# Mixer of a two-layer diffusion backbone: two attention heads side by side on halves of the array, projections ranked ahead, no modulation dots in the mixer

## The chip, the cores and the metric

The kernel runs on one core of one Trainium2 chip. The metric is device time in microseconds of that core for one launch; lower is better. The core's engines are TensorE (PE in the profile, with PEld for its weight loads), VectorE (DVE), ScalarE (ACT), GpSimd (POOL) and SyncE (SP, which issues the DMAs). They run beside each other, each through its own queue in order, and are tied together by semaphores.

## The reference, cut to what matters

There are 256 latent tokens and 256 context tokens, 1024 features and two layers. Layer 0 is a half-step SwiGLU, then a mixer of windowed attention and a gated linear attention (GLA), then another half-step SwiGLU. Layer 1 is a SwiGLU, a pooling mixer, a SwiGLU. Each norm is modulated by columns that come from a conditioning vector: nine vectors of 1024 a layer, each a matrix-vector product. The change lies in the mixer of layer 0 and in the place of some of those products.

```python
def adaln(cond, w, b):                       # 9 modulation vectors of 1024 for a layer
    mm = jax.nn.silu(cond) @ w + b
...
def window_attention(q, k, v, kc, vc, sink): # 8 query heads of 64, 2 key/value heads of 64
    s_band = jnp.einsum('bnigrd,bnjgd->bgrnij', qb, kb).astype(jnp.float32) * scale
    s_ctx = jnp.einsum('bnigrd,blgd->bgrnil', qb, kc).astype(jnp.float32) * scale
    s_band = jnp.where(valid, s_band, -jnp.inf)
    p = jax.nn.softmax(jnp.concatenate([s_band, s_ctx, sink_l], axis=-1), axis=-1)
    o = (jnp.einsum('bgrnij,bnjgd->bnigrd', p[..., :nk], vb)
         + jnp.einsum('bgrnil,blgd->bnigrd', p[..., nk:nk + L], vc))
...
def gla_chunked(q, k, v, log_a, s0):         # 4 heads of 64 x 128, chunks of 64, both directions
    g = jnp.cumsum(chunks(log_a), axis=2)
    q_t = qc_ * jnp.exp(g)
    k_t = kc_ * jnp.exp(-g)
    att = jnp.where(lower, jnp.einsum('bnihd,bnjhd->bnhij', q_t, k_t), 0.0)
    o = jnp.einsum('bnhij,bnjhv->bnihv', att, vc_)
    ...
    o = o + jnp.einsum('bnihd,bnhdv->bnihv', q_t, s_prev)
```

## The kernel before, in words

Activations lie feature by token: 128 features on the partitions, 256 tokens along the free axis. Weights come from HBM in blocks of 128 x 1024 (512 KB). `weight` (L139 to L146) loads such a block into one of four `raw` buffers, ScalarE casts it to `hi` (L144), and VectorE subtracts to get `lo` (L145); each product is then three matmuls (`product`, L327 to L329, on 258 columns; `wide`, L342 to L344; `merged`, L336 and L337). The matmuls inside the mixer that concern this change are plain fp32 matmuls; the trace shows two records for each of them.

The stages follow one another: the two-stream SwiGLU of layer 0 (`ffn_two`), the mixer (`mixer`), the second SwiGLU of layer 0 and the first of layer 1 (`ffn_one`: 22 blocks p of two weights, then eight output blocks), the pooling mixer, the last SwiGLU. In `ffn_one` the blocks p below 9 use `product` and the later ones `wide`.

A modulation column is made by a *dot*: VectorE multiplies a 128 x 1024 weight tile by the conditioning row and sums it (L174). `queue_mod` lists the dots in order; `step_mod(rate)` does so many of them per step of a stage and keeps two loads ahead. In the SwiGLUs the weight tiles go into two buffers of their own (`rawm`); in the mixer they use the four `raw` buffers. The rates of the second SwiGLU of layer 0 and the first of layer 1 are the first two pairs of `RATES` (dots for each block p from 5 on, and for each output block). In the mixer one dot follows each projection named in `DOTS`: ten in all.

The mixer's order of work is written by a small planner, `Flow`. Each piece of work is a generator; `step(pe, post, needs, sets)` tells the planner what it costs on PE, which VectorE ("D") and ScalarE ("A") work follows, and which events it needs and sets. The planner always continues the ready task with the lowest rank (`RANK`), and a task whose `post` work is not done is not ready. The order that comes out is then laid on the engines by the recording layer, which moves some instructions of its own. The tasks are:

- `project`: 19 blocks of the input projection (`ORDER`), each one or two times 24 matmul records of `product`, then L374 on VectorE and L766 on ScalarE;
- `gate`: decays, and from them `k_t`, `q_t` (GLA keys and queries); `q_t` has one slot a head, its other 64 rows zero;
- `scores(d, tb)`: GLA scores, four 128 x 128 matmuls a call over all 128 rows (L971);
- `states`: GLA states (L951), two heads on the two halves of the array's columns, alternating;
- `gla_head`: a head's output, per half of the tokens one L984, four L989 (64 columns each, all 128 rows), one L991; then its norm, which goes through a matmul of ones (L999);
- `attend(j, g, qb, u)`: one head and one query block: scores (L904, 128 x 512, `k_g` zero in the other head's 64 rows), VectorE (L907 to L909), ScalarE (L910, L911), VectorE (L912 to L914), four transposes (L921), a ScalarE copy (L922), and after the second query block four value matmuls (L931) into the half of a bank that belongs to the head's group g. There are 16 of them, and three P buffers (`PBUF`) let three be under way;
- `output`: eight output blocks with `merged`.

Of the kernel before, what the change touches and what calls it, by code (L numbers as in the profile page):

```python
# [13 lines left out]
ALU = mybir.AluOpType  # L14
# [44 lines left out]
RANK = dict(gate=0, small=1, scores=3, states=3, gla=2, attend=2, output=5, project=10)  # L59
# [47 lines left out]
class Body:  # L107
# [597 lines left out]
    def mixer(self, cur, nxt):  # L705
# [12 lines left out]
        k_g = t(lp, [128, 2, 512])  # L718
        k_t = t(lp, [128, 2, 2, T])
        q_t = t(lp, [128, 2, 4, T])  # L720
# [4 lines left out]
        for z in (k_g, q_t, KT):  # L725
            nc.gpsimd.memset(z, 0.0)
# [67 lines left out]
        def rope(blk):  # L794
# [7 lines left out]
            if blk == "ka":  # L802
                for g in (0, 1):
                    r = slice(g * 64, g * 64 + 64)
                    nc.vector.tensor_tensor(k_g[r, g, :T], t1[r], t2[r], op=ALU.add)
                    nc.scalar.copy(k_g[r, g, T:], z[r, T:])
            else:
                nc.vector.tensor_tensor(q_r[:, int(blk[2]), :], t1, t2, op=ALU.add)
# [13 lines left out]
        def gate(d, b):  # L822
# [32 lines left out]
            for hh in (0, 1):  # L855
                r = slice(hh * 64, hh * 64 + 64)
                nc.vector.scalar_tensor_tensor(out=q_t[r, d, 2 * b + hh, :], in0=Z[f"qb{b}"][r], scalar=0.125,
                                               in1=ep[r], op0=ALU.mult, op1=ALU.mult)
# [37 lines left out]
        pv_bank, pv_last, PT = {}, {}, {}  # L896

        def attend(j, g, qb, u):


            h = g * 4 + j
            sk = self.cols[:, C_SK + h:C_SK + h + 1]
            ps = self.bank()
            nc.tensor.matmul(ps, q_r[:, j, qb * 128:(qb + 1) * 128], k_g[:, g, :], start=True, stop=True)  # L904
            p = t(sp, [128, 512], F32, "P", PBUF)
            st = t(sp, [128, 4], F32, "st", 4)
            nc.vector.tensor_tensor_reduce(out=p, in0=ps, in1=band[:, qb, :], scale=0.125, scalar=sk,  # L907
                                           op0=ALU.add, op1=ALU.max, accum_out=st[:, 0:1])
            nc.vector.tensor_scalar_mul(st[:, 1:2], st[:, 0:1], -1.0)  # L909
            nc.scalar.activation(st[:, 3:4], sk, AF.Exp, bias=st[:, 1:2])  # L910
            nc.scalar.activation(p, p, AF.Exp, bias=st[:, 1:2], accum_out=st[:, 2:3])  # L911
            nc.vector.tensor_tensor(st[:, 2:3], st[:, 2:3], st[:, 3:4], op=ALU.add)  # L912
            nc.vector.reciprocal(st[:, 2:3], st[:, 2:3])
            nc.vector.tensor_scalar_mul(p, p, st[:, 2:3])  # L914
            yield step(0.86, [("D", ATT[0]), ("A", ATT[1]), ("D", ATT[2])])
            if qb == 0:
                PT[h] = t(sp, [128, 4, T], F32, "PT", 2)
            pt = PT[h]
            pk = self.bank()
            for kb in range(4):  # L920
                nc.tensor.transpose(pk[:, kb * 128:(kb + 1) * 128], p[:, kb * 128:(kb + 1) * 128], self.ident)  # L921
            nc.scalar.copy(pt[:, :, qb * 128:(qb + 1) * 128], pk.rearrange("p (k q) -> p k q", q=128))  # L922
            yield step(0.44, [("A", 0.48)], sets=[f"T{u}"])
            if qb == 0:
                return
            if j not in pv_bank:
                pv_bank[j] = self.bank()
            po = pv_bank[j]
            with self.after(pv_last.get(j)):
# [112 lines left out]
        for d in (0, 1):  # L1042
            for tb in (0, 1):
                flow.add(RANK["scores"], scores(d, tb), [f"qk{d}0", f"qk{d}1"])
# [243 lines left out]
```

## Time and profile before

| what | us |
|---|---|
| median of 3 runs (1159.35 to 1163.1) | 1162.02 |
| the profiled execution: its own time | 1161.4 |
| the profiled execution: span of its instructions | 1159.2 |
| PE busy | 1137.5 |
| DVE busy | 938.5 |
| ACT busy | 587.4 |
| mixer, from the first projection on PE to the start of the next SwiGLU's blocks | 391.87 to 564.11 |
| second SwiGLU of layer 0, `product` blocks, then `wide` blocks | 564.11 to 618.48, to 693.35 |
| first SwiGLU of layer 1, `product` blocks, then `wide` blocks | 755.54 to 807.78, to 882.65 |

The span runs from the first to the last instruction; 2.2 us of the execution lie outside of it. The granted TensorE clock is full (0.997 in the mean). In a row of the timeline the first number is the start, the second the length up to the modelled end of the last instruction, and "xN" counts records; since matmuls are pipelined, the cost of a block is the distance from its start to the start of what follows. Rows of groups give the busy sum, the mean of one instruction in ns, and the idle time before them with what ended it. A row of the windows gives the stretch, its length, and for PE, PEld, DVE, ACT and POOL the busy time in it with the count of instructions; then the clock, the DMA engines' share and GB/s.

### The profile page before, as it was taken

The page shows a single profiled execution, that of the slowest core. Times are in us where ns is not written, and L with a number is a line of the kernel's source. Part 1 is how long each engine was busy: PE and PEld are TensorE (multiplying, and loading weights), DVE is VectorE, ACT ScalarE, POOL GpSimd, SP SyncE. Part 2 cuts the span into 40 slices and gives each one's busy share as a digit, 9 for nine tenths or more (in the row PEclk, how much of TensorE's full clock was granted, in tenths as well). Part 3 has the DMA queues.
Part 4 walks back from the last instruction along what each step waited for, and adds up shares of the span by engine and source line. Part 5 has one row for each costly group of instructions (what it writes and reads, how often), then busy time and mean ns, then how long its engine had stood idle before and what let it go on. Part 6 is the DMA issues. An engine that isn't in the chain of part 4 may idle for free.

```text
span 1159.2 us, 19546 instructions
## 1 busy us (share of the span) xinstructions
PE 1137.5 (98%) x7450; PEld 1027.0 (89%) x7450; DVE 938.5 (81%) x1662; ACT 587.4 (51%) x999; POOL 9.9 (1%) x32
## 2 busy tenths in 40 slices
PE   7999999999999999999999999999999999999997
PEld 5899988888888899787999998899999889988886
DVE  6899899787758889776999877989886889967664
ACT  4547645323234474565574444565544556556543
POOL 0000000000000200000000000000000000000000
PEclk9999999999999999999999999999999999999998
DMA  9867557667866535321759977868996864756562
GB/s 332 289 243 240 164 179 233 198 217 243 249 191 191 171 108 177 115 69 54 234 187 324 326 236 246 283 208 284 340 312 203 261 226 147 252 185 192 153 185 88
DMA packets 74544, 247.42 MB, mean 213 GB/s; under 512 B 8273, under 2 KB 8913, under 8 KB 74194
## 3 DMA queue, kind: packets, MB, share of 16 engines
q1 hardware_dynamic: 74450, 246.17, 64.4%
q8 instruction: 58, 0.95, 0.3%
q14 instruction: 36, 0.29, 0.1%
HBM read 245.09 MB, written 1.05 MB: 212 GB/s over the span
## 4 chain that ended last, share of the span: by engine, by line
PE 86%; DVE 7%; DMA 3%; ACT 2%; issue 2%; SPq 0%; DVEq 0%; ACTq 0%
PE t_mm L336 15%; PE t_mm L342 11%; PE t_mm L344 11%; PE t_mm L343 11%; PE t_mm L337 8%; PE t_mm L329 7%; PE t_mm L328 7%; PE t_mm L327 7%; PE t_mm L610 2%; DVE t_lo L145 1%; PE t_mm L931 1%; PE t_mm L904 1%; DVE t_junk L174 1%; DMA t_x<-ctxT 1%; ACT t_hi L144 1%
## 5 line engine op out<-in xcount | busy, mean ns | idle before, releaser
L144 ACT CAST t_hi<-t_raw 128x1024 fp32r<-128x1024 f32 (+1 forms) x344 | 326.0, 950 | 368.2 <-PE t_mm L343 160.8
L145 DVE TENSOR_TENSOR t_lo<-t_raw,t_hi 128x1024 fp32r<-128x1024 f32 (+1 forms) x344 | 376.6, 1097 | 87.2 <-ACT t_hi L144 84.1
L327 PE MATMUL t_mm<-t_xA,t_hi 128*128 128x258 f32 (+1 forms) x912 | 261.0, 287 | 2.7 <-DVE t_x L957 1.6
L329 PE MATMUL t_mm<-t_xA,t_lo 128*128 128x258 f32 (+1 forms) x912 | 259.6, 285 | 3.1 <-DVE t_lo L145 3.1
L328 PE MATMUL t_mm<-t_xA,t_hi 128*128 128x258 f32 (+1 forms) x912 | 258.1, 283 | 0.1
L174 DVE CUSTOM_DVE_ANT_0 t_junk<-t_rawm,t_x 128x1024 bf16<-128x1024 f32 x142 | 181.7, 1280 | 23.8 <-DMA t_rawm<-wmod 22.9
L336 PE MATMUL t_mm<-t_g,t_hi 128*128 128x512 f32 x528 | 186.6, 398 | 0.0
L344 PE MATMUL t_mm<-t_xA,t_lo 128*128 128x256 f32 (+1 forms) x592 | 186.2, 315 | 0.0
L342 PE MATMUL t_mm<-t_xA,t_hi 128*128 128x256 f32 (+1 forms) x592 | 186.2, 315 | 0.0
L343 PE MATMUL t_mm<-t_xA,t_hi 128*128 128x256 f32 (+1 forms) x592 | 186.2, 315 | 0.0
L327 PEld LDWEIGHTS t_mm<-t_xA,t_hi 128*128 128x128 f32 x912 | 173.0, 190 | 5.9 <-DVE t_x L957 1.9
L329 PEld LDWEIGHTS t_mm<-t_xA,t_lo 128*128 128x128 f32 x912 | 172.6, 189 | 4.2 <-DVE t_lo L145 4.2
L328 PEld LDWEIGHTS t_mm<-t_xA,t_hi 128*128 128x128 f32 x912 | 172.7, 189 | 2.4 <-issue 1.4
L337 PE MATMUL t_mm<-t_g,t_lo 128*128 128x256 f32 x528 | 147.9, 280 | 0.0
L336 PEld LDWEIGHTS t_mm<-t_g,t_hi 128*128 128x128 f32 x528 | 99.2, 188 | 23.8
L343 PEld LDWEIGHTS t_mm<-t_xA,t_hi 128*128 128x128 f32 x592 | 112.9, 191 | 6.9
L344 PEld LDWEIGHTS t_mm<-t_xA,t_lo 128*128 128x128 f32 x592 | 112.9, 191 | 6.9
L342 PEld LDWEIGHTS t_mm<-t_xA,t_hi 128*128 128x128 f32 x592 | 112.9, 191 | 6.7
L337 PEld LDWEIGHTS t_mm<-t_g,t_lo 128*128 128x128 f32 x528 | 99.7, 189 | 0.0
L336 PE MATMUL t_mm<-t_xA,t_hi 128*128 128x512 f32 x272 | 95.4, 396 | 0.0
L337 PE MATMUL t_mm<-t_xA,t_lo 128*128 128x256 f32 x272 | 75.4, 278 | 0.0
L342 PE MATMUL t_mm<-t_g,t_hi 128*128 128x512 f32 x176 | 68.5, 389 | 0.0
(244 smaller groups left out, 1388.7 us busy)
## 6 DMA issues: line engine op xcount, KB each, us to landing
t_raw<-wi SPq DMA_DIRECT2D x190, 512.0 KB, 4.6
t_rawm<-wmod SPq DMA_DIRECT2D x118, 512.0 KB, 4.5
t_raw<-wo SPq DMA_DIRECT2D x64, 384.0 KB, 3.6
t_raw<-wo SPq DMA_DIRECT2D x64, 320.0 KB, 3.3
t_raw<-win SPq DMA_DIRECT2D x18, 512.0 KB, 3.7
t_w<-wmod SPq DMA_DIRECT2D x16, 512.0 KB, 6.6
t_raw<-wmod SPq DMA_DIRECT2D x10, 512.0 KB, 4.3
t_raw<-wi0k SPq DMA_DIRECT2D x8, 512.0 KB, 6.3
```

The costliest lines, as they stand in the source:

```text
L144: nc.scalar.copy(hi[:, :n], raw[:, :n])
L145: self.mark = nc.vector.tensor_tensor(lo[:, :n], raw[:, :n], hi.bitcast(F32)[:, :n], op=ALU.subtract)
L174: self.nc.vector.tensor_tensor_reduce(out=junk, in0=w, in1=self.srow[s], scale=0.5 if half else 1.0, scalar=b, op0=ALU.mult, op1=ALU.add, ...
L327: nc.tensor.matmul(ps[:, :n], hi[:, c], X[:, 0, k, :n], start=(k == 0), stop=False)
L328: nc.tensor.matmul(ps[:, :n], hi[:, c], X[:, 1, k, :n], start=False, stop=False)
L329: nc.tensor.matmul(ps[:, :n], lo[:, c], X[:, 0, k, :n], start=False, stop=(k == KB - 1))
L336: nc.tensor.matmul(ps, hi, X.rearrange("p x t -> p (x t)"), start=first, stop=False)
L337: nc.tensor.matmul(ps[:, T:], lo, X[:, 0], start=False, stop=last)
L342: nc.tensor.matmul(ps, hi, X0, start=first, stop=False)
L343: nc.tensor.matmul(ps, hi, X1, start=False, stop=False)
L344: nc.tensor.matmul(ps, lo, X0, start=False, stop=last)
L610: nc.tensor.matmul(ps[i][:, :T], w[:, i * 128:(i + 1) * 128], xf[:, k, :], start=(k == 0), stop=(k == KB - 1))
```

## The change

In words:

- Attention works on two heads at once, one of each key/value group. `k_g` is one tile of 128 rows (64 of each group); the two score matmuls of 64 rows stand one behind the other, on the lower and the upper half of the array's rows, each into its own bank. VectorE and ScalarE do the same large operations for two heads in a row, and the small ones once for both. The eight value matmuls of a pair alternate between the two halves of the columns. There are eight units in place of 16, four P buffers, so two units under way; the value bank is taken when it is used and not held across two heads.
- GLA scores use 64 rows a head, two heads one behind the other, in two calls of two banks in place of four calls. `q_t` has no zero halves. In `gla_head` the L989 matmuls (L991 in the new file) use the 64 rows of their head alone: always the same half within one head, between matmuls over all 128 rows.
- Planner: projections get rank 4, ahead of attention and GLA outputs (5); scores and states stay at 3.
- `DOTS` is empty: the mixer does no dots. The rates of the two SwiGLUs behind it rise from 1.35 and 1.4 to 1.6 and 1.6, which places the ten dots: four more in the blocks p of the second SwiGLU of layer 0, one more in its output; four more in the blocks p of the first of layer 1, two more in its output; and one fewer in the last SwiGLU. The total is the same.
- Three zero fills shrink to one, `ka` is written with two operations in place of four, `q_t` with one in place of two.

```diff
-RATES = ((1.35, 1.4), (1.35, 1.4), (0.9, 0))
+RATES = ((1.6, 1.6), (1.6, 1.6), (0.9, 0))
...
-PBUF = 3
+PBUF = 4
+SC, PVT = 0.9, 1.0
...
-DOTS = "ka va vb0 vb1 vb2 qa0 qa2 qa3 rb0 rb1".split()
+DOTS = ()
...
-RANK = dict(gate=0, small=1, scores=3, states=3, gla=2, attend=2, output=5, project=10)
+RANK = dict(gate=0, small=1, scores=3, states=3, project=4, gla=5, attend=5, output=6)
...
+            ps = [self.bank() for _ in (0, 1)]
+            for g in (0, 1):
+                nc.tensor.matmul(ps[g], q_r[rows(g), j, qb * 128:(qb + 1) * 128], k_g[rows(g), :], start=True, stop=True)
+            P = [t(sp, [128, 512], F32, "P", PBUF) for _ in (0, 1)]
...
+            for g in (0, 1):
+                nc.vector.tensor_tensor_reduce(out=P[g], in0=ps[g], in1=band[:, qb, :], scale=0.125, scalar=sk[g],
+                                               op0=ALU.add, op1=ALU.max, accum_out=st[:, 0, g:g + 1])
+            nc.vector.tensor_scalar_mul(st[:, 1, :], st[:, 0, :], -1.0)
+            for g in (0, 1):
+                nc.scalar.activation(st[:, 3, g:g + 1], sk[g], AF.Exp, bias=st[:, 1, g:g + 1])
+                nc.scalar.activation(P[g], P[g], AF.Exp, bias=st[:, 1, g:g + 1], accum_out=st[:, 2, g:g + 1])
...
+            po = self.bank()
+            for kb in range(4):
+                for g in (0, 1):
+                    nc.tensor.matmul(po[rows(g), :T], v_sb[:, kb, rows(g)], PT[j][g][:, kb, :],
+                                     start=(kb == 0), stop=(kb == 3))
...
-            for h in range(4):
-                nc.tensor.matmul(ps[:, h * 128:(h + 1) * 128], k_t[:, d, h // 2, c], q_t[:, d, h, c],
-                                 start=True, stop=True)
+            ps = [self.bank() for _ in (0, 1)]
+            for i, (tb, b) in enumerate(((0, 0), (0, 1), (1, 0), (1, 1))):
+                c = slice(tb * 128, (tb + 1) * 128)
+                for hh in (0, 1):
+                    nc.tensor.matmul(ps[hh][:, i * 128:(i + 1) * 128], k_t[rows(hh), d, b, c], q_t[rows(hh), d, b, c],
+                                     start=True, stop=True)
...
-                            nc.tensor.matmul(po[:, cc], S[:, d, ch, h // 2, :], q_t[:, d, h, cc],
+                            nc.tensor.matmul(po[:, cc], S[r, d, ch, h // 2, :], q_t[r, d, h // 2, cc],
```

What the planner and the recording layer make of it on PE. In the middle of the attention, before: the end of a GLA head's output (L984, L989, L991), one head's value matmuls (L931), one head's transposes (L921) and two heads' scores (L904).

```order
L984 MATMUL t_mm<-t_x 128x128
L989 MATMUL t_mm<-t_x 128x64 x4
L991 MATMUL t_mm<-t_x 128x128
L931 MATMUL t_mm<-t_PT,t_x 64x256 x4
L921 MATMUL t_mm<-t_x,t_P 128x128 x4
L904 MATMUL t_mm<-t_x 128x512 x2
```

The same place now (L986, L991 and L993 are the GLA head's matmuls in the new file, L932 the values, L924 the transposes, L904 again the scores):

```order
L986 MATMUL t_mm<-t_x 128x128
L991 MATMUL t_mm<-t_x 128x64 x4
L993 MATMUL t_mm<-t_x 128x128
L932 MATMUL t_mm<-t_PT,t_x 64x256 x8
L924 MATMUL t_mm<-t_x,t_P 128x128 x8
L904 MATMUL t_mm<-t_x 128x512 x2
```

One block of values now serves two heads, so four such blocks stand on PE in place of eight; the two L904 are one pair. The projections have not all moved ahead: a projection task is not ready again until its own VectorE and ScalarE work is done in the plan, and attention still fills those times. So it goes on PE after the third unit of attention in the new file (L797 is a rope matmul, L947 the states, L904 the fourth unit's scores, L924 the third unit's transposes):

```order
L797 MATMUL t_mm<-t_z_4661,t_x 128x256
L947 MATMUL t_mm<-t_x 64x128 x20
L904 MATMUL t_mm<-t_x 128x512 x2
L924 MATMUL t_mm<-t_x,t_P 128x128 x8
L328 MATMUL t_mm<-t_xA,t_hi 128x258
L329 MATMUL t_mm<-t_xA,t_hi 128x258
L330 MATMUL t_mm<-t_xA,t_lo 128x258
```

Behind these rows stand the rest of the 24 matmuls of that projection, then the fifth unit's scores and at once the fourth unit's transposes: what lies between a pair's scores and its transposes is one pair's transposes, one projection and one pair's scores. Before, the last projection stands ahead of the scores of the last four heads; now it stands ahead of those of the last two units, which are four heads too.

On VectorE, in the second SwiGLU of layer 0 at block p = 6, before: one dot (the L174 rows: the product and the read of its sum) among a block's evacuation (L374, L366) and casts (L145).

```order
L174 ISA t_junk,t_x<-t_rawm,t_x 128x1024
L174 ISA t_x 128x1
L374 TENSOR_TENSOR t_zu<-t_mm,t_rstd 128x257
L145 TENSOR_TENSOR t_lo<-t_raw,t_hi 128x1024
L366 SCALAR_TENSOR_TENSOR t_za<-t_zu,t_za 128x256
L374 TENSOR_TENSOR t_za<-t_mm,t_rstd 128x257
L145 TENSOR_TENSOR t_lo<-t_raw,t_hi 128x1024
```

Now, at the same block (one line further down in the new file):

```order
L175 ISA t_junk,t_x<-t_rawm,t_x 128x1024
L175 ISA t_x 128x1
L375 TENSOR_TENSOR t_zu<-t_mm,t_rstd 128x257
L175 ISA t_junk,t_x<-t_rawm,t_x 128x1024
L175 ISA t_x 128x1
L367 SCALAR_TENSOR_TENSOR t_za<-t_zu,t_za 128x256
L375 TENSOR_TENSOR t_za<-t_mm,t_rstd 128x257
L146 TENSOR_TENSOR t_lo<-t_raw,t_hi 128x1024
```

A second dot stands ahead of the block's evacuation and cast.

More of the change, by code (lines that the diff above doesn't have):

```diff
@@ L717, in mixer @@
         q_r = t(lp, [128, 4, T])
-        k_g = t(lp, [128, 2, 512])
+        k_g = t(lp, [128, 512])
         k_t = t(lp, [128, 2, 2, T])
-        q_t = t(lp, [128, 2, 4, T])
+        q_t = t(lp, [128, 2, 2, T])
         s_r = t(lp, [128, 4, T])
@@ L724, in mixer @@
         KC = t(lp, [128, 2, 2, 256])
-        for z in (k_g, q_t, KT):
-            nc.gpsimd.memset(z, 0.0)
+        nc.gpsimd.memset(KT, 0.0)
         cs = t(zp, [128, 2, T])
@@ L802, in rope @@
             if blk == "ka":
[L803 to L806, printed above, removed]
+                nc.vector.tensor_tensor(k_g[:, :T], t1, t2, op=ALU.add)
+                nc.scalar.copy(k_g[:, T:], z[:, T:])
             else:
@@ L854, in gate @@
             nc.vector.tensor_copy(decay[:, d, b, :], ev[:, :, edge])
[L855 to L858, printed above, removed]
+            nc.vector.scalar_tensor_tensor(out=q_t[:, d, b, :], in0=Z[f"qb{b}"], scalar=0.125, in1=ep,
+                                           op0=ALU.mult, op1=ALU.mult)
             nc.vector.tensor_tensor(k_t[:, d, b, :], Z[f"kb{b}"][:, :T], en, op=ALU.mult)
@@ L894, in split @@
             nc.vector.tensor_tensor(O[:, k, 1], src, O.bitcast(F32)[:, k, 0], op=ALU.subtract)
[L896 to L915, printed above, removed]
-            if qb == 0:
[L917 to L923, printed above, removed]
@@ L924, in attend @@
             if qb == 0:
                 return
[L926 to L929, printed above, removed]
-                for kb in range(4):
-                    ins = nc.tensor.matmul(po[g * 64:(g + 1) * 64, :T], v_sb[:, kb, g * 64:(g + 1) * 64],
-                                           pt[:, kb, :], start=(kb == 0), stop=(kb == 3))
-            second = j in pv_last
-            pv_last[j] = ins
@@ L935, in attend @@
-            if second:
-                split(j, po[:, :T])
-                yield step(1.72, [("A", 0.31), ("D", 0.34)], sets=[f"a{h}", f"o{j}"])
-            else:
-                yield step(1.72, sets=[f"a{h}"])
+            po = self.bank()
+            for kb in range(4):
+                for g in (0, 1):
+                    nc.tensor.matmul(po[rows(g), :T], v_sb[:, kb, rows(g)], PT[j][g][:, kb, :],
+                                     start=(kb == 0), stop=(kb == 3))
+            split(j, po[:, :T])
@@ L941, in vb @@
+            yield step(PVT, [("A", 0.4), ("D", 0.42)], sets=[f"o{j}"])
         def vb(tb, c):
@@ L979, in gla_head @@
             c = slice(h * 128, (h + 1) * 128)
+            r = rows(h % 2)
             prev = None
@@ L1042, in mixer @@
         for d in (0, 1):
-            for tb in (0, 1):
-                flow.add(RANK["scores"], scores(d, tb), [f"qk{d}0", f"qk{d}1"])
+            flow.add(RANK["scores"], scores(d), [f"qk{d}0", f"qk{d}1"])
         for d in (0, 1):
@@ L1048, in mixer @@
         for h in range(4):
[L1049 removed]
+            flow.add(RANK["gla"], gla_head(h), [f"S{d}{h // 2}" for d in (0, 1)] + [f"att{d}" for d in (0, 1)]
                      + [f"sr{h}"])
[L1051 to L1054 removed]
+        for u, (j, qb) in enumerate((j, qb) for j in range(4) for qb in (0, 1)):
+            need = ["tka", "tva", f"tqa{j}"] + ([f"T{u - PBUF // 2}"] if u >= PBUF // 2 else [])
+            flow.add(RANK["attend"], attend(j, qb, u), need)
         flow.add(RANK["output"], output(), ["rb3"])
```

33 lines of the change are left out of this document (22 added, 11 removed).

## The prediction

> **What bounds the kernel now.** I read the page first. Its head and its first part say that TensorE is the bound on the whole:
>
> ```profile
> span 1159.2 us, 19546 instructions
> PE 1137.5 (98%) x7450; PEld 1027.0 (89%) x7450; DVE 938.5 (81%) x1662; ACT 587.4 (51%) x999; POOL 9.9 (1%) x32
> ```
>
> An average hides stages, so next came the windows, cut where PE passes from one kind of matmul to another: the mixer's attention (two rows), and the SwiGLU blocks that take over the dots.
>
> ```profile
> 464.46:502.74 38.28, 38.28 (x265) 30.06 (x264) 29.27 (x89) 23.46 (x54) 0.00 (x0) 1.00 0.35 111
> 502.74:546.52 43.78, 43.78 (x274) 33.89 (x273) 29.13 (x85) 24.09 (x59) 0.15 (x2) 1.00 0.11 37
> 564.11:618.48 54.37, 53.48 (x435) 52.81 (x435) 51.73 (x90) 33.73 (x52) 0.00 (x0) 1.00 0.68 221
> 618.48:693.35 74.87, 74.87 (x626) 74.87 (x626) 61.82 (x98) 35.28 (x54) 0.18 (x3) 1.00 0.86 298
> 807.78:882.65 74.87, 74.87 (x626) 74.87 (x626) 62.21 (x100) 34.90 (x53) 0.00 (x0) 1.00 0.88 304
> ```
>
> In the 82.06 us of attention PE never rests, at full clock, while VectorE works 58.4 us and ScalarE 47.6. So PE time taken out there is time won as long as the other two keep up: they have some 24 and 34 us to spare. In the SwiGLU blocks PE is full too, but VectorE has only 13 us free of 74.87, and 2.6 of 54.37 in the earlier blocks. PE's waits over the mixer are one entry. The chain of waits shows what came ahead of it:
>
> ```profile
> PE t_mm L327 <- DVE t_x L957: 1.6, 1, 1.6
> ...
> 456.03 1.20 DVE t_junk L174
> 458.08 1.04 ACT t_hi L144
> 459.14 1.23 DVE t_lo L145
> ```
>
> **The change part by part.** The terms on PE come from the timeline, start of a block to start of what follows it:
>
> ```profile
> 443.69 3.74 PE L971 MATMUL t_mm<-t_x 128*128 128x128 f32 x32
> 447.18 0.36 PE L327 MATMUL t_mm<-t_xA,t_hi 128*128 128x258 f32 x1
> ...
> 477.93 1.94 PE L931 MATMUL t_mm<-t_PT,t_x 128*64 128x256 f32 x8
> 479.80 2.84 PE L904 MATMUL t_mm<-t_x 128*128 128x512 f32 x6
> 482.57 2.40 PE L951 MATMUL t_mm<-t_x 128*64 128x128 f32 x40
> 484.90 0.66 PE L921 MATMUL t_mm<-t_x,t_P 128*128 128x128 f32 x4
> ...
> 502.91 1.00 PE L989 MATMUL t_mm<-t_x 128*128 128x64 f32 x8
> 503.75 0.44 PE L991 MATMUL t_mm<-t_x 128*128 128x128 f32 x2
> ```
>
> and their counts from the groups:
>
> ```profile
> L904 PE MATMUL t_mm<-t_x 128*128 128x512 f32 x32 | 15.6, 599 | 0.0
> L931 PE MATMUL t_mm<-t_PT,t_x 128*64 128x256 f32 x64 | 15.5, 385 | 0.0
> L989 PE MATMUL t_mm<-t_x 128*128 128x64 f32 x64 | 8.0, 268 | 0.0
> L989 PEld LDWEIGHTS t_mm<-t_x 128*128 128x128 f32 x64 | 7.8, 192 | 0.0
> ```
>
> What side by side is worth: L971 has full-width matmuls of 128 columns, 3.49 us for 32 records, 0.109 each. L951 has the same 128 columns on halves of the array's columns, two heads alternating: 2.33 us for 40 records, 0.058 each. So two halves together cost 0.53 of one after the other. This row is for halves of the columns; no row has halves of the rows. The bounds there are 0.53 and 1.0. I take 0.53, since alternating halves is what L951 does too.
>
> What a change between whole and half costs: the chain of waits lists a block of four score records without such a change, and it takes 0.43 a record.
>
> ```profile
> 516.18 1.72 PE t_mm L904 x4
> ```
>
> The block at 479.80 stands between two half-array blocks: 2.77 us for six records, 0.19 more than 6 x 0.43. I take 0.2 for going in and out.
>
> - Values: eight blocks of 8 records, 1.87 us each, are 15.0 us. Four blocks of 16 alternating records cost 4 x 16 x 0.234 x 0.53 = 7.9 (1.87 / 8 = 0.234). Gain 7.1.
> - Attention scores: 32 records x 0.43 = 13.8. Side by side 7.3, and seven blocks that go in and out (the first two units share one) 1.4. Gain 5.1.
> - GLA scores: 3.49, side by side 1.85 and one going in and out 0.2. Gain 1.4.
> - GLA outputs: the L989 block of 8 records is 0.84 us, eight such blocks. Their rows are halved, not their columns, and one head uses one half, so nothing runs side by side. Each block now goes in and out: 8 x 0.2 = 1.6 lost (0 to 1.6 as the row allows).
>
> PE in sum: 7.1 + 5.1 + 1.4 - 1.6 = 12.0 us less.
>
> PE's one wait of 1.6 us comes from VectorE, whose copy of a state (L957) stood behind a dot at 456.03 and a cast at 459.14, which itself waited for ScalarE's cast at 458.08. With no dots, and the four raw buffers left to the weights, it shrinks by 0 to 1.6; I take half, 0.8.
>
> Against this, attention's own chain. Per head:
>
> ```profile
> L907 DVE CUSTOM_DVE_ANT_0 t_P<-t_mm,t_x 128x512 f32<-128x512 f32 x16 | 11.9, 747 | 5.7 <-PE t_mm L904 5.7
> L907 DVE DVE_READ_ACCUMULATOR2_ANT t_st<- 128x1 f32 x16 | 1.3, 82 | 0.0
> L909 DVE TENSOR_SCALAR t_st<-t_st 128x1 f32<-128x1 f32 x16 | 2.4, 149 | 0.2
> L910 ACT ACTIVATE t_st<-t_x,t_st 128x1 f32<-128x1 f32 x16 | 4.7, 292 | 8.7 <-DVE t_st L909 8.6
> L911 ACT ACTIVATE t_P<-t_P,t_st 128x512 f32<-128x512 f32 x16 | 11.3, 709 | 0.0
> L911 ACT ACTIVATION_READ_ACCUMULATOR t_P<-t_P,t_st 128x1 f32 x16 | 3.0, 187 | 0.0
> L912 DVE TENSOR_TENSOR t_st<-t_st 128x1 f32<-128x1 f32 x16 | 2.5, 155 | 1.9 <-ACT t_P L911 1.7
> L913 DVE RECIPROCAL t_st<-t_st 128x1 f32<-128x1 f32 x16 | 2.6, 160 | 0.2
> L914 DVE TENSOR_SCALAR t_P<-t_P,t_st 128x512 f32<-128x512 f32 x16 | 7.7, 483 | 0.3
> ```
>
> One head takes 2.96 us from scores to normalized P. A pair takes 2 x 0.829 + 0.149, then 2 x 1.188, then 0.155 + 0.160 + 2 x 0.483: 5.47 us. In the new order the tightest unit (the fourth) has between its scores and its transposes one pair's transposes (8 records; the L921 block at 484.90 has 4 in 0.66), one projection of 24 records and one pair's scores. A projection's records start 0.12 apart:
>
> ```profile
> 485.77 0.28 PE L328 MATMUL t_mm<-t_xA,t_hi 128*128 128x258 f32 x1
> 485.89 0.28 PE L329 MATMUL t_mm<-t_xA,t_lo 128*128 128x258 f32 x1
> ```
>
> So the cover is at most 1.3 + 2.9 + 1.1 = 5.3 us against 5.47 and what is queued on VectorE and ScalarE for that projection. What waits behind such a transpose is everything on PE. Bounds: nothing (no wait in the two attention rows before) to 0.75 in each of the eight units, 6 us. I take 2.5.
>
> The dots: ten leave the mixer, where VectorE was no bound but for that one wait, so their leaving wins nothing else. One costs 1.28 us, and the read of its sum 0.08 as L907's does. Behind the mixer the second SwiGLU of layer 0 gets four more in its blocks. VectorE there: 61.82 + 4 x 1.36 = 67.3 of 74.87, hidden by PE. DMA: 298 GB/s x 74.87 us = 22.3 MB and 4 x 0.52 MB make 24.4, 326 GB/s; at a share of 0.86 for 298 that is 0.94. Hidden, barely. The earlier blocks get one more: 51.73 + 1.36 = 53.1 of 54.37, with 0.9 us of PE idle there already. The narrowest place is the two buffers for the dots' weights:
>
> ```profile
> L174 DVE CUSTOM_DVE_ANT_0 t_junk<-t_rawm,t_x x16: 1277/1280/1286, 619.0 to 678.7; 128x1024 bf16<-128x1024 f32 x16
> DMA t_rawm<-wmod: 3.4, 5
> DMA to landing us min/median/max: 4.3/5.1/6.1
> ```
>
> A buffer's cycle is a dot of 1.36 and a landing of 5.1, 6.5 us: with two buffers one dot in 3.2 us at best, in 3.7 with the longest landing. A block is 48 matmuls of 0.12, 5.76 us; at a rate of 1.6 it asks for one in 3.6. Every late load holds up VectorE's queue, and the weight casts of the next block, for which PE waits, stand behind it; SP's next weight loads stand behind a dot's load that waits for its buffer. VectorE already waits 3.4 us here without PE feeling it. For the two stages together I take 1.2 us on PE, with bounds of 0 and 6. The one dot fewer in the last SwiGLU wins nothing: VectorE does not bound PE there. The smaller zero fills, `ka` and `q_t` writes lie on engines with room: 0.
>
> Sum: 1161.4 - 12.0 - 0.8 + 2.5 + 1.2 = 1152.3 for a profiled execution. The median of the runs shown is 0.6 above the profiled one, so the forecast is 1152.9.
>
> The Trainium skill, page "TensorE: Matmul & The Clock Gate", Part 3 (Measured speedup vs the span model), gives 3.07 times for four quarters of the rows; half of that for two halves, 1.54, is an estimate from that page, a factor of 0.65 in place of 0.53, and the score terms would then gain 2.1 us less: 1155.0. No run here shows it yet.
>
> **The rivals.**
>
> *Half rows don't run side by side.* For it: no row of the trace has them. Against it: half columns do. Then both score terms keep their length and pay for going in and out: 1.4 + 0.2 lost instead of 6.5 gained, so PE gains 12.0 - 8.1 = 3.9; the chain has more cover (no wait), the other terms stay: 1161.4 - 3.9 - 0.8 + 1.2 + 0.6 = 1158.5. Chance 0.08.
>
> *Slower: weight loads in the half-row GLA matmuls come out from under the matmuls.* Today the L989 records start 0.84 / 8 = 0.105 apart though a weight load shows 0.192 and a matmul 0.268, so a load runs under the matmul ahead of it. If within one half of the rows each load had to wait for that matmul's end, a record would take 0.46, 64 x 0.355 = 22.7 us more: 1175.6. It decides from 0.14 us a record, where the gain of 9.1 is gone. Against it: L931 before also loads and multiplies in one half (of the columns) again and again, 0.234 a record of 256 columns. Chance 0.07.
>
> By the Trainium skill, page "TensorE: Matmul & The Clock Gate", Part 3 (The mechanism), loads overlap running matmuls only when the group of rows differs. L989's spacing, with all rows in every matmul, speaks against that as a general rule.
>
> *The SwiGLU stages take the gain back.* If the two buffers, or VectorE, set the pace of the two stages, up to their bound of 6 us and as much again from later loads of weights: 1153 + 5 to 10, about 1159. For it: 3.2 to 3.7 against 3.6. Against: PE is 74.87 of 74.87 in both with the dots they have. Chance 0.10.
>
> *The pairs' chain bounds attention.* With two units under way, waits of 8 us or more: 1159. For it: 5.47 against 2.96 with fewer under way. Against: room on both engines, and other work between. Chance 0.08.
>
> **How the numbers follow.** The forecast has 0.67, its own range 1147 (every PE term, no going in and out in the GLA heads, the whole 1.6, no waits: 12.0 + 1.6 + 1.6 off 1162) to 1158. A measurement of this kernel can tell about 0.3% from no change, so faster ends at 1158.5 and slower begins at 1165.5. Faster: 0.67, and 0.04 of the first rival, 0.03 of the third, 0.01 of the fourth: 0.75. Within 0.3%: 0.04 + 0.07 + 0.06 = 0.17. Slower: 0.07, and 0.01 of the fourth (waits of 13 us): 0.08. The range of 1147 to 1161 leaves out the second rival and the far ends of the third and fourth, some 0.16.
>
> **What would show it.** In the profile after: the score blocks of two matmuls at about 0.9 us and 0.2, the value blocks of 16 records at about 2.0, L989's successor still near 0.11 a record; attention, from the first scores to the last values, shorter by 8 to 12 us; PE's waits in it a few us, on VectorE's L914 or ScalarE; the wide SwiGLU blocks at 74.9 us still. It is wrong if a score pair takes 1.7, if the 64-column matmuls take 0.2 or more each, or if the wide blocks pass 77 us.

## The result, and the profile after

The change makes the kernel faster: 1153.14 us (median of 8, 1151.67 to 1159.89) against 1161.01 us (8), ratio 0.9937 with a 95% interval of 0.9918 to 0.9957. That is 7.9 us; the forecast was 1152.9.

Two executions of the changed kernel were profiled. The first, with a time of 1159.89 us, is the longest of its eight. The second, "again" below, with 1150.46 us, is the shortest of its six. Views of after are of "again" unless said otherwise; where the two differ is itself a finding. The head of its page:

```profile
span 1148.7 us, 19496 instructions
PE 1127.0 (98%) x7450; PEld 1019.5 (89%) x7450; DVE 931.7 (81%) x1633; ACT 586.2 (51%) x998; POOL 7.3 (1%) x30
```

PE is as full as before, with 10.5 us less to do. The windows of before, cut anew: from the first GLA score to the end of the last value matmul ("attention" below), and from there to the end of the matmul of the next SwiGLU's norm ("output stage" below). That matmul stands behind the first block of the next SwiGLU, so this stage ends later than the 564.11 of the table of before.

```profile
443.69:546.47 102.78, 101.14 (x715) 82.45 (x713) 76.55 (x210) 55.81 (x127) 0.89 (x3) 1.00 0.31 102
546.47:570.92 24.45, 24.00 (x151) 21.48 (x151) 21.74 (x41) 15.78 (x28) 0.00 (x0) 1.00 0.64 216
```

The same two stretches after, and the `wide` blocks of the second SwiGLU of layer 0:

```profile
441.80:529.95 88.15, 87.61 (x703) 73.70 (x702) 61.49 (x161) 52.69 (x123) 0.15 (x2) 1.00 0.22 69
529.95:558.75 28.80, 26.88 (x163) 23.07 (x161) 23.83 (x46) 16.40 (x30) 0.00 (x0) 1.00 0.57 183
606.25:681.68 75.43, 75.13 (x627) 74.92 (x625) 63.69 (x104) 33.40 (x51) 0.18 (x3) 1.00 0.89 310
```

Attention is 14.6 us shorter, the output stage 4.3 us longer. Some of both is only a boundary that moved: before, 28 of the 128 `merged` records and the last norm's matmul stood ahead of the last values, now 20 and not the norm (8 x 0.177 + 0.35 = 1.8 us). The mixer as a whole, which has no such boundary, went from 179.11 us (391.81 to 570.92) to 168.92 (389.83 to 558.75): 10.2 less.

The timeline of after, blocks from start to what follows: GLA scores (L970), values (L932), a score pair (L904), states (L947), transposes (L924), and half of a GLA head (L986, L991, L993).

```profile
441.80 2.06 PE L970 MATMUL t_mm<-t_x 64*128 64x128 f32 x32
443.79 0.39 PE L328 MATMUL t_mm<-t_xA,t_hi 128*128 128x258 f32 x1
...
472.97 1.95 PE L932 MATMUL t_mm<-t_PT,t_x 128*64 128x256 f32 x16
474.85 1.13 PE L904 MATMUL t_mm<-t_x 64*128 64x512 f32 x4
...
479.43 2.40 PE L947 MATMUL t_mm<-t_x 128*64 128x128 f32 x40
481.93 1.32 PE L904 MATMUL t_mm<-t_x 64*128 64x512 f32 x4
...
487.11 1.13 PE L904 MATMUL t_mm<-t_x 64*128 64x512 f32 x4
488.63 1.06 PE L924 MATMUL t_mm<-t_x,t_P 128*128 128x128 f32 x8 [0.40 <-DVE t_P L917]
...
492.44 0.38 PE L986 MATMUL t_mm<-t_x 128*128 128x128 f32 x2
492.76 1.10 PE L991 MATMUL t_mm<-t_x 64*128 64x64 f32 x8
493.79 0.49 PE L993 MATMUL t_mm<-t_x 128*128 128x128 f32 x2
494.12 0.39 PE L986 MATMUL t_mm<-t_x 128*128 128x128 f32 x2
...
498.78 1.13 PE L904 MATMUL t_mm<-t_x 64*128 64x512 f32 x4
499.84 0.39 PE L328 MATMUL t_mm<-t_xA,t_hi 128*128 128x258 f32 x1
```

Sixteen value records take 1.88 us where eight took 1.87. A score pair takes 1.06 us (498.78 to 499.84). GLA scores take 1.99 where they took 3.49. The states' blocks take 2.50 (the one shown) and 2.45; before they took 2.34 and, with the wait, 4.05. The wait is gone. Half a GLA head takes 1.68 us (492.44 to 494.12); before it took 1.34.

PE's waits from the start of the mixer to 900 us, late in the first SwiGLU of layer 1, in "again" (us in total, times, longest):

```profile
PE t_mm L330 <- DVE t_lo L146: 2.3, 4, 1.0
PE t_mm L924 <- DVE t_P L917: 0.4, 1, 0.4
PE t_mm L345 <- DVE t_lo L146: 0.3, 1, 0.3
PE t_mm L338 <- DVE t_lo L146: 0.3, 1, 0.3
```

The attention chain is the second row, 0.4 us in all. The others are all of one kind: VectorE's `lo` part of a weight is late. In the first profiled execution that kind is larger, in the `wide` blocks above all:

```profile
PE t_mm L345 <- DVE t_lo L146: 3.3, 6, 0.9
PE t_mm L330 <- DVE t_lo L146: 1.9, 3, 1.0
```

There the two `wide` stretches take 78.15 and 77.24 us, against 75.43 and 74.99 in "again" and 74.87 and 74.88 before. The other difference is the granted clock. In the first it falls to 0.86 from 490 to 500 us, in attention, and to 0.89 and 0.94 from 940 to 960 us, ahead of the last SwiGLU; in "again" it is full there. Attention takes 89.82 us in the first, 1.7 more, and the stretch from the end of layer 1's first SwiGLU to the start of the last one's blocks 24.77 us against 22.49. So of the 9.4 us between the two executions some 4.0 lie where the clock fell, 4.4 are the SwiGLUs, and 1.0 lies ahead of the mixer.

So the theory to test: the mixer wins 10.2 us by half-array pairs and by the wait at the states, less what GLA heads and a late output stage cost; the moved dots give some us back in the SwiGLUs, more in some executions than in others. The rivals: the pairs win by fewer starts and ends of blocks and not by running side by side; or the gain is the dots' and not the pairs'.

### The profile page after: what moved, and what is told of

The parts are those of the page before. It is cut to its first block, busy times and chain, and to the rows that moved or that the text cites. A ratio compares the mean times of both kernels' runs of the same rounds, so it can differ in the third digit from the quotient of the medians.

```text
span 1158.1 us, 19496 instructions
## 1 busy us (share of the span) xinstructions
PE 1132.5 (98%) x7450; PEld 1022.7 (88%) x7450; DVE 931.2 (80%) x1633; ACT 586.5 (51%) x998; POOL 7.3 (1%) x30
## 4 chain that ended last, share of the span: by engine, by line
PE 71%; DMA 11%; DVE 10%; ACT 4%; issue 3%; SPq 0%; DVEq 0%; ACTq 0%
PE t_mm L337 15%; PE t_mm L345 8%; PE t_mm L338 8%; PE t_mm L344 8%; PE t_mm L343 8%; PE t_mm L330 6%; DMA t_raw<-wi 6%; PE t_mm L329 6%; PE t_mm L328 6%; DVE t_lo L146 3%; DMA t_rawm<-wmod 3%; PE t_mm L611 2%; DVE t_junk L175 2%; ACT t_hi L145 2%; PE t_mm L932 1%
## 5 line engine op out<-in xcount | busy, mean ns | idle before, releaser
L145 ACT CAST t_hi<-t_raw 128x1024 fp32r<-128x1024 f32 (+1 forms) x344 | 325.7, 950 | 371.5 <-PE t_mm L344 121.5
L175 DVE CUSTOM_DVE_ANT_0 t_junk<-t_rawm,t_x 128x1024 bf16<-128x1024 f32 x152 | 194.5, 1279 | 22.1 <-DMA t_rawm<-wmod 21.2
```

The lines of the kernel that those rows point to most:

```text
L145: nc.scalar.copy(hi[:, :n], raw[:, :n])
L175: self.nc.vector.tensor_tensor_reduce(out=junk, in0=w, in1=self.srow[s], scale=0.5 if half else 1.0, scalar=b, op0=ALU.mult, op1=ALU.add, ...
```

## The experiments

All ratios are to the kernel before, run beside each experiment, with a median of 1161.0 to 1161.5 us. A difference between two kernels is given as the difference of their ratios times 1161. The interval of each ratio is 1.2 to 2.1 us wide to either side, so differences of about 2 us and less are not clear of the noise by the times alone; for these the stages of the profile decide, and each profile is of one execution.

**The change once more.**

> The changed kernel once more, since its profiled execution (1159.9 us) stood 6.7 us above its median. Theory: the mixer is the same to a few tenths (the attention from the first GLA scores to the last values about 90 us, the output about 28 us up to the second SwiGLU's second block), and what made that execution long lies in the two wide stretches of the SwiGLUs behind it (78.2 and 77.2 us there, 74.9 before the change) and in the pooling mixer; in a usual execution they take 75 to 76.5. About 1153 us. Rival: the profiled execution is how the kernel always runs inside, and the other executions are short for another reason: the wide stretches are at 77 to 78 again.

Measured: 1154.01 us (1150.46 to 1154.88), ratio 0.9935 (0.9921 to 0.9949). The result stands. The profile above is of this run.

**Half rows undone.** Attention and GLA scores over all 128 rows against zeros, in the change's order:

```diff
-                nc.tensor.matmul(ps[g], q_r[rows(g), j, qb * 128:(qb + 1) * 128], k_g[rows(g), :], start=True, stop=True)
+                nc.tensor.matmul(ps[g], q_r[:, j, qb * 128:(qb + 1) * 128], k_g[:, g, :], start=True, stop=True)
...
-                    nc.tensor.matmul(ps[hh][:, i * 128:(i + 1) * 128], k_t[rows(hh), d, b, c], q_t[rows(hh), d, b, c],
+                    nc.tensor.matmul(ps[hh][:, i * 128:(i + 1) * 128], k_t[:, d, b, c], q_t[:, d, 2 * b + hh, c],
```

> The change with the matmuls of the attention scores and of the GLA scores over all 128 rows again, against zeros in the other head's rows (attention order, pairs of heads, value matmuls, dots as in the change). Theory: a pair of attention scores takes 1.72 us in place of about 0.9 and 0.2, the GLA scores 3.5 in place of 2.0, so 5 to 7 us are lost less what the longer cover saves in waits: 1157 to 1160. Rival (halves of the rows gain nothing, the pairing and the order do): 1152 to 1154.

Measured: 1158.86 us, ratio 0.9982 (0.9972 to 0.9992), 5.5 us slower than the change. The GLA scores' block in its timeline:

```profile
443.94 3.74 PE L975 MATMUL t_mm<-t_x 128*128 128x128 f32 x32
447.43 0.36 PE L328 MATMUL t_mm<-t_xA,t_hi 128*128 128x258 f32 x1
```

3.49 us again, and the attention scores' blocks go from 8.93 us in sum to 12.45. The mixer is 5.7 us longer, which is the whole slowdown. Half rows do run side by side: in the change the two heads' records of a pair start 7 ns apart.

**The values' alternation undone**, the largest term of the prediction:

```diff
-            for kb in range(4):
-                for g in (0, 1):
+            for g in (0, 1):
+                for kb in range(4):
```

> The change with one thing turned round: in each of the four value blocks the four matmuls of the first head run one after the other and then the four of the second, where the change alternates the heads. Theory: two matmuls on different halves of the array's columns run side by side only when they stand next to each other; without the alternation only the seam between the heads overlaps, a block of 8 matmuls goes from 1.88 us to 3.3 to 3.7 us, the four blocks from 7.5 to about 14, and the time from 1153.9 to about 1159.5 (1157.5 to 1161.5; not the whole 6.5 where a value block covers a chain that is waited for anyway). Rival: the value blocks became shorter because one block of 8 took the place of two blocks of 4 and saved their starts and ends, not by running side by side: the blocks stay at 1.9 to 2.3 us and the time at 1153.9 +- 1.

Measured: 1157.07 us, ratio 0.9963 (0.995 to 0.9976), 3.3 us slower than the change. A block:

```profile
473.56 2.86 PE L932 MATMUL t_mm<-t_PT,t_x 128*64 128x256 f32 x16
476.35 1.13 PE L904 MATMUL t_mm<-t_x 64*128 64x512 f32 x4
```

2.79 us, half way between 1.88 and twice 1.87: neither theory had it. The starts of the 16 records, in us from the block's start, by head, from the trace:

```
first head   0.000 0.266 0.482 0.698 0.914 1.130 1.345 1.561
second head  0.920 1.186 1.402 1.618 1.834 2.050 2.265 2.481
```

The second head starts with the fifth record of the first, though three records stand ahead of it in the queue; from there the two run side by side, 6 ns apart at first. So the overlap is real, but it does not need neighbours: here the two halves ran side by side with four records between them. Whether four is a limit no run shows. Four blocks cost 3.6 us more, close to the measured slowdown, so the edit takes back about half of what the values won, and not all of it.

**The dots back in the mixer**, and, turned round, **the dots alone** taken out of the kernel before (the same two lines of that file, the other way):

```diff
-RATES = ((1.6, 1.6), (1.6, 1.6), (0.9, 0))
+RATES = ((1.35, 1.4), (1.35, 1.4), (0.9, 0))
...
-DOTS = ()
+DOTS = "ka va vb0 vb1 vb2 qa0 qa2 qa3 rb0 rb1".split()
```

> The change with the ten dots back in the mixer and the rates of before. Theory (the gain is PE time saved by halves of the array; moving the dots is worth nothing or costs): the wait behind the states comes back with up to 1.6 us, the wide stretches return to 74.9 each; 1150 to 1153 us, no slower than the change by more than 1 us. Rival (the gain comes from taking the dots out of the mixer): most of the gain is lost, 1157 to 1161.

Measured: 1151.23 us, ratio 0.9918 (0.9905 to 0.9931), 2.0 us faster than the change; the intervals overlap.

> The kernel before with the dots alone moved (none in the mixer, rates of 1.6). Theory: the mixer wins its one wait of 1.6 us, the wide stretches lose 1 to 6 us; 1160 to 1165. Rival (taking the dots out earns the gain): 1153 to 1157.

Measured: 1164.62 us, ratio 1.0023 (1.0012 to 1.0034), slower than before by 2.7 us, clear of the noise. In its profile the wait behind the states is gone, and the `wide` stretches take 76.15 and 75.54 us. With the dots back in the change, the wait behind the states is back too:

```profile
PE t_mm L328 <- DVE t_x L953: 1.7, 1, 1.7
```

and the mixer takes 170.37 us, 1.45 more. But the `wide` stretches are 74.87 and 74.87 again. In the two profiled executions the two cancel (1150.46 us each); in the medians the SwiGLUs seem to lose more. So this part of the change is a loss, of 2 to 3 us by the medians, and the rival that the gain is the dots' falls.

**Three buffers for the dots' weights** in the two SwiGLUs:

```diff
-            w = self.t(self.modpool, [128, 1024], F32, "rawm", 2)
+            w = self.t(self.modpool, [128, 1024], F32, "rawm", self.rawm_bufs)
```

> The change, with three buffers in place of two for the modulation weights that the two wide SwiGLU stages load. Theory: the dots that were moved there are late because a weight load can only start when the dot two before it is done, and VectorE then waits for the load with the lo parts of the product's weights queued behind it; with three buffers the wide stretches of the second and third stage go back to 74.9 each (75.4 and 75.0 in a usual execution of the change, up to 78.2 and 77.2), TensorE's waits for t_lo there vanish, and the time goes from 1153.9 to about 1152.5 (1151.5 to 1153.3), most of the 2 us that dots_back won. Rival: the dots' cost is VectorE's own time in these stages and not the wait for buffers: unchanged, 1153.9 +- 0.6.

Measured: 1151.9 us (1149.91 to 1154.61), ratio 0.9922 (0.9907 to 0.9938), 1.5 us faster than the change; the intervals overlap. The two `wide` stretches:

```profile
607.52:682.53 75.01, 75.01 (x627) 74.96 (x625) 64.74 (x106) 34.25 (x53) 0.18 (x3) 1.00 0.89 318
797.69:872.56 74.87, 74.87 (x626) 74.87 (x625) 65.09 (x105) 34.24 (x53) 0.00 (x0) 1.00 0.91 324
```

VectorE does the same dots (64.74 us busy where the dots in the mixer leave 61.5) and PE does not wait. What VectorE waited for in the first `wide` stretch: in the first profiled execution of the change,

```profile
DVE t_lo L146 <- ACT t_hi L145: 9.7, 9, 2.6
DVE t_junk L175 <- DMA t_rawm<-wmod: 3.4, 5, 2.0
```

and with three buffers the second row is not there. The row's sum alone proves nothing: it is 3.4 us before and 4.1 with the dots back in the mixer, and PE does not wait in either. What differs is its longest wait: 1.0 and 1.3 us there, 1.3 in "again", 2.0 here, and 2.7 in the version with a new order below, where the first `wide` stretch takes 78.03. The number of buffers is the better evidence. With the moved dots and two buffers the first `wide` stretch takes 75.4 to 78.2 us in the seven profiles (five versions and the two of the change); with three buffers it takes 75.01, 74.88 and 75.48 in three versions. So most of the cost is the wait for a buffer, with the `lo` parts queued behind it, and not VectorE's work; the 75.48 (PE waits 0.2 us for a `lo` part there, without a wait for a buffer) says that it is not all. That three buffers also make the time steady is not shown: its executions still spread over 4.7 us.

**GLA heads over all rows**: the 64-column matmuls as before, the scores as in the change.

```diff
-                            nc.tensor.matmul(po[:, cc], S[r, d, ch, h // 2, :], q_t[r, d, h // 2, cc],
+                            nc.tensor.matmul(po[:, cc], S[:, d, ch, h // 2, :], q_t[:, d, h, cc],
```

> The change, with the 64-column matmuls of the four GLA heads over all 128 rows again (q_t of each head with zeros in the other half, as in the kernel before); scores and values stay on half rows. Theory: the half rows gain nothing in a block that is alone on its half, and going in and out of them costs about 0.31 us in each of the eight half-heads; so the eight 64-column records take 0.84 us again where the change shows 1.03, the two neighbours 0.22 and 0.28 where it shows 0.31 and 0.32, the stretch from the GLA scores to the end of the last values goes from 88.2 to about 85.8, and the time from 1153.9 to about 1151.5 (1150.5 to 1153). Rival (the blocks hang on their operands, not on the rows): the records' spacing goes back but the stretch does not shorten, 1153.9 +- 0.6.

Measured: 1148.97 us (1147.96 to 1150.37), ratio 0.9899 (0.9884 to 0.9915), 4.2 us faster than the change. Half a head:

```profile
493.23 0.38 PE L989 MATMUL t_mm<-t_x 128*128 128x128 f32 x2
493.45 1.00 PE L994 MATMUL t_mm<-t_x 128*128 128x64 f32 x8
494.29 0.44 PE L996 MATMUL t_mm<-t_x 128*128 128x128 f32 x2
494.57 0.39 PE L989 MATMUL t_mm<-t_x 128*128 128x128 f32 x2
```

1.34 us again, and the mixer takes 165.96 us, 3.0 less: 2.3 in attention as expected, 0.7 in the output stage. The other 1.2 us of the gain are in no stage that the edit touches; they stay open, and are within the noise.

**The last GLA head's norm earlier**, by one move in the order of the projections:

```diff
-ORDER = "kb0 qb1 zg qb0 kb1 ka va vb0 vb1 qa0 vb2 qa1 vb3 qa2 rb0 rb1 qa3 rb2 rb3".split()
+ORDER = "kb0 qb1 zg qb0 kb1 ka va vb0 vb1 qa0 vb2 qa1 vb3 qa2 rb0 rb1 rb2 qa3 rb3".split()
```

It was made because of the place of the norm's matmul of ones. In before's timeline (L999) it stands ahead of both last value blocks; in after's (L1001) it stands behind the last:

```profile
540.87 0.60 PE L999 MATMUL t_mm<-t_osq,t_x 128*128 128x256 f32 x2
541.39 1.94 PE L931 MATMUL t_mm<-t_PT,t_x 128*64 128x256 f32 x8
...
544.60 1.94 PE L931 MATMUL t_mm<-t_PT,t_x 128*64 128x256 f32 x8
```

```profile
528.08 1.95 PE L932 MATMUL t_mm<-t_PT,t_x 128*64 128x256 f32 x16
529.96 0.70 PE L1001 MATMUL t_mm<-t_osq,t_x 128*128 128x256 f32 x2
530.30 0.58 PE L337 MATMUL t_mm<-t_xA,t_hi 128*128 128x512 f32 x1
```

> The change, with the projection of qa3 moved behind that of rb2, so that the attention pairs of j = 3 come after the last GLA head's start and not ahead of it. Theory: the 4.3 us by which the output stage grew (24.5 to 28.8) are the last GLA head's norm, which the change puts behind the last values, so that the k = 7 product of the first output group ends late, its weight buffers come free late and the later groups wait for their lo parts; with the norm ahead of the last values the output stage takes 24.5 to 25.5 and its 104 last matmuls stand in one row. The pairs of j = 3 then have fewer projections to cover their chains: 0 to 2 us back in attention. Time 1153.9 - 3.5 + 1 = about 1151.4 (1149.8 to 1153.5). Rival: the output stage grew because its weights are loaded later against the end of attention, whatever the norm does: output stage 28 to 29 still and 1154 to 1156.

Measured: 1151.93 us, ratio 0.9917 (0.9905 to 0.993), 2.1 us faster than the change; the intervals overlap. Its attention and output stage:

```profile
442.39:533.16 90.77, 89.31 (x709) 74.51 (x708) 63.08 (x165) 53.65 (x125) 0.15 (x2) 1.00 0.20 66
533.16:557.70 24.54, 24.54 (x157) 22.08 (x155) 22.39 (x43) 15.49 (x28) 0.00 (x0) 1.00 0.72 236
```

The output stage is back at 24.54 and PE has no wait left in it. Attention takes 2.6 more, of which 1.1 is the boundary again (four `merged` records and the norm's matmul); most of the rest is the chain of P, which has fewer projections to hide behind:

```profile
PE t_mm L924 <- DVE t_P L917: 1.1, 2, 0.7
```

Net, the mixer is 1.6 us shorter. The edit moves the norm, but with it qa3 and its pairs, so that the late norm is the cause is supported by the place where the time came back, not isolated.

**Combinations.** First the dots in the mixer, GLA heads over all rows, and the new place of qa3:

> The change with three things at once: the dots and rates of the kernel before, the GLA heads' 64-column matmuls over all rows, and qa3 projected behind rb2. If the three costs are each what the theory says and lie in different places (wide stages, attention, output stage), they add: 1153.9 - 2.8 - 2.4 - 2.5 = about 1146.2 (1144.5 to 1149). If the dots, back in the mixer, fall into the stretch that the new order has made tighter, or a saving only moves a wait, 1149 to 1152.

Measured: 1147.59 us (1145.88 to 1152.07), ratio 0.9889 (0.9871 to 0.9907). That is 5.3 us faster than the change, where the three alone make 2.0 + 4.2 + 2.1 = 8.3. The output stage is right (24.31 us) and the two `wide` stretches take 74.88 each, but the mixer takes 168.39 us where the three edits by their own profiles make 165.8. Attention, and ten us of it:

```profile
443.72:535.82 92.10, 88.37 (x709) 74.93 (x708) 71.30 (x184) 55.29 (x127) 0.15 (x2) 0.98 0.32 114
460.00:470.00 10.00, 9.52 (x57) 8.12 (x58) 7.71 (x22) 2.41 (x5) 0.00 (x0) 0.83 0.45 162
```

The granted clock is 0.83 there, and the projection of 24 records in these ten us takes 4.48 us in place of 3.00: 1.5 of the missing 2.6 is the clock of this execution. The wait behind the states (2.0 us) and the chain of P (1.0) are no loss of the combination: the dots in the mixer alone have the first with 1.7, and the new order alone the second with 1.1. New are 0.3 more at the states and a wait of 0.5 us behind the GLA scores, for VectorE's evacuation of a projection. The median lies inside the range of the first case, that the three add; whether a saving also became a wait, as the second case said, is not shown. Then the dots out of the mixer with three buffers, GLA heads over all rows, without and with the new place of qa3:

> The change with two mends: the GLA heads' 64-column matmuls over all rows and three buffers for the modulation weights; the order of the projections is the change's. If they add: mixer 166.0 (as with the full-row GLA heads alone), wide stretches 74.9 each, about 1147.7 (1146.5 to 1149.5), above the version with the new place of qa3 by the 1.6 us that the order gained in the mixer. Rival: the two versions come out equal, since the order's gain in the output stage is taken back in attention.

Measured: 1147.31 us, ratio 0.9881 (0.9867 to 0.9894). This differs from the version with GLA heads over all rows by the three buffers alone, and is 2.1 us faster than it; alone on the change the buffers gave 1.5.

> The change with the three mends that each showed a gain and do not touch one another: the GLA heads' 64-column matmuls over all rows, three buffers for the modulation weights of the wide SwiGLU stages, and qa3 projected behind rb2; the dots stay out of the mixer. If they add: mixer 168.9 - 3.0 - 1.6 = 164.3, wide stretches 74.9 each, product stretches 46.1 to 46.8; against the change's 1153.9 that is about 1147 by the profiles of the three (-2.9, -1.5 to -3, -1.6) and 1146 to 1148.5 by range. Rival: with the GLA heads shorter, the pairs of j = 3 behind them lose cover and give 1 to 2 us back in attention: 1148 to 1149.

Measured: 1144.21 us (1143.48 to 1145.2), ratio 0.9854 (0.9841 to 0.9867): faster than before by 17.0 us and than the change by 9.4. Attention, the output stage and the two `wide` stretches:

```profile
442.96:531.07 88.11, 86.65 (x710) 73.36 (x709) 63.74 (x167) 54.94 (x126) 0.45 (x3) 1.00 0.23 77
531.07:555.60 24.53, 24.53 (x157) 22.06 (x155) 22.38 (x43) 15.60 (x28) 0.00 (x0) 1.00 0.76 256
601.67:676.54 74.87, 74.87 (x626) 74.87 (x625) 65.16 (x107) 34.59 (x52) 0.18 (x3) 1.00 0.91 319
791.52:866.40 74.88, 74.88 (x627) 74.88 (x625) 65.14 (x104) 34.50 (x54) 0.00 (x0) 1.00 0.91 322
```

The three mends add: 4.2 + 1.5 + 2.1 = 7.8 by their own ratios, 9.4 together, which puts the time below the range expected (1146 to 1148.5 us); the 1.6 us over the sum are within the noise of the ratios. The order's gain is 3.1 us here, so the rival that attention takes it back falls.

No run changes the ranks of the planner or the number of P buffers alone, so their own share in the result is not isolated.

## Why the prediction was right, point by point

The total was right, and its mechanism too: PE bounds, and half-array pairs take time from it. Its sum for the mixer was 12.0 + 0.8 - 2.5 = 10.3 us; measured 10.2. That they agree so closely is partly luck, since several terms were off in both directions. The 0.2 us between forecast and median are luck too: the forecast took 9.1 us off a median of 1162.0, and the change took 7.9 off one of 1161.0. Blocks of before against "again", in us:

| term | predicted | measured | from |
|---|---|---|---|
| values | -7.1 | -7.5 | blocks of 14.97, now 7.51 |
| attention scores | -5.1 | -4.4 | 12.1, now 8.5 without the wait, and 0.8 net in the `product` blocks |
| GLA scores | -1.4 | -1.5 | 3.49, now 1.99 |
| GLA heads in and out of half rows | +1.6 | +2.8 | 10.81, now 13.56 |
| wait behind the states | -0.8 | -1.4 | 6.39, now 4.95 |
| attention chain | +2.5 | +0.5 | a score block of 1.53 against 1.06 |
| output stage's `merged` blocks | 0 | +1.6 | 23.20, now 24.81 |
| transposes, norms and small matmuls | 0 | -0.2 | the rest |
| dots in the two SwiGLUs | +1.2 | +1.9 here, +6.3 in the other execution | `product` and `wide` stretches |

- *Side by side.* The factor of 0.53 came from L951, a row of column halves, and stood for row halves as well. It was slightly too high: pairs on halves cost 0.50, and 0.2 for going in and out. The estimate from the Trainium skill (page "TensorE: Matmul & The Clock Gate", Part 3, Measured speedup vs the span model), 1.54 times for two halves, worked out from its 3.07 for four quarters, is not what happens here. Two pairs in a row take 1.92 us and one 1.06, so a pair costs 0.86 where two whole-array heads take 1.72: 2.0 times. The attention term was over-sized all the same, since its "before" was counted as 32 x 0.43 = 13.8, and the trace has 12.1 in the blocks and 0.8 behind them. One pair of the eight, right behind the states, starts 0.20 us apart and takes 1.25.
- *GLA heads.* The step "Each block now goes in and out: 8 x 0.2" was mis-sized: it is 0.34 a block, 2.8 in all, beyond its bounds of 0 to 1.6. The sign was right, and the full-row experiment shows that undoing it wins.
- *The wait behind the states* went wholly, where half was taken; with the dots back it returns, so the dots caused it.
- *The attention chain* was mis-sized, 0.5 for 2.5: of the eight units one waits. Counted as the prediction counted its 82.06 us, from the first attention scores, attention went to 70.43 (459.53 to 529.96): 11.6 us shorter, 9.9 without the boundary, inside the 8 to 12 named. That "the cover is at most 5.3 us against 5.47" made the shortage one of tenths, and the value taken was a guess between far ends.
- *The output stage* was not in the sum. The step that failed is the unwritten one that everything behind the last values stays as it was. The new order puts the last GLA head behind the last transposes, and its norm behind the last values, which could have been read from the order of PE.
- *The dots* cost more than 1.2 in the median, and the cause named, two buffers with the `lo` parts queued behind a late load, is supported by the runs with three. One reading was wrong: the first `wide` stretch got three dots more (19 for 16) and not four, and VectorE is busy 63.7 us there, not 67.3. Against the statement that PE would be covered in 74.9 stand 75.0 to 78.2. That the wide blocks "pass 77 us", given as a sign of being wrong, came true in one of the two executions. The rival "the SwiGLU stages take the gain back" is thus there in part: 6.3 us in that execution, about its bound of 6, and 1.9 in the other.
- The rival of half rows one after the other falls by the whole-row experiment. The slower one, loads that come out from under the half-row GLA matmuls, falls too: within a block their records start 0.112 us apart, as over whole rows.

Of the 10.5 us between the two spans, 2.0 lie ahead of the mixer, where the change does nothing. There the start of the mixer varies from 389.6 to 391.9 us over the profiles without following the edit (the dots moved alone in the kernel before: 389.6; three buffers: 391.9), so this is no part of the gain.

## What to carry to other kernels

A matmul that uses half of the array is worth it only when something runs on the other half; alone it saves nothing and pays for the way in and out, so pair the heads where two are at hand and keep whole rows where one stands alone. When a stage gets shorter, look at what ends last now, at the small tasks at its seam above all (here a norm of two records), and read that from the new order of the bottleneck engine. Before moving work to an engine "with room", count the buffers that feed it: what matters is what stands behind its waits, not its busy share.

## What the runs showed of the hardware

- Two fp32 matmuls on different halves of the array, rows or columns, start 6 to 7 ns apart (0.20 us in one pair, right behind the states) and each then runs at its own pace: a pair of 64 x 512 score matmuls costs 0.86 us for two heads, and one whole-array head 0.86 too.
- TensorE started a matmul of the free half while three records of the busy half still stood ahead of it in its queue (the values without alternation: 2.79 us a block, not 3.7). So its queue was not worked off strictly in order.
- The price of going from whole rows to half rows and back lies in the records at the seam. In a GLA half-head of after the first two of the L991 records come 0.205 and 0.160 us after the one ahead, against 0.109 and 0.059 before; the two of the matmul behind come 0.202 and 0.213 after, against 0.111 and 0.165. In between nothing is lost: 0.112 both times. The Trainium skill, page "TensorE: Matmul & The Clock Gate", Part 3 (The mechanism), says that a weight load overlaps running matmuls only where the group of rows differs; here eight matmuls of one half, each with its own load of 0.19 us, run 0.112 us apart as before, so the measurement speaks against the rule.
- Executions of one kernel can differ by some us at the same work: the change ran from 1150.5 to 1159.9 us, and of the 9.4 us some 4.0 lie where the granted clock fell to 0.86 to 0.94. In the first combination a projection of 24 records took 4.48 us in place of 3.00 in ten us at a clock of 0.83. The last version stayed within 1143.5 to 1145.2 us, but in four executions only.
